# Series of unread matrix products, at many addresses, behind the last store of an encoder kernel

## The chip, the cores and the metric

The kernel runs on one core of a Trainium2 chip. The metric is the device time of one execution, in microseconds (us). TensorE (PE) multiplies; VectorE (DVE), ScalarE (ACT) and GpSimd (POOL) work on its sums and on tiles in SBUF; SyncE (SP) issues all the kernel's DMAs. PEld stands for TensorE's weight loads.

## The reference

Two layers of an encoder over 256 tokens of width 1024. Each layer adds, in turn, to the residual x: half a SwiGLU feed-forward (inner width 2816), three token mixers side by side, a cross-attention into 256 memory tokens, and half a second feed-forward; a norm ends the layer.

```python
for l in range(DEPTH):                                   # DEPTH = 2
    x = x + 0.5 * swiglu(rms_norm(x, ffn1_norm[l]), ffn1_w_in[l], ffn1_w_out[l])
    z = rms_norm(x, mix_norm[l]) @ w_mix_in[l]
    o_mla, o_swa, o_na = mla_mixer(z...), swa_mixer(z...), na_mixer(z...)
    x = x + concat(rms_norm(o_mla), rms_norm(o_swa), rms_norm(o_na)) @ w_mix_out[l]
    x = x + mem_xattn(rms_norm(x, mem_norm_x[l]), mem, ...)
    x = x + 0.5 * swiglu(rms_norm(x, ffn2_norm[l]), ffn2_w_in[l], ffn2_w_out[l])
    x = rms_norm(x, block_norm[l])
return x
```

## The kernel before

Activations lie transposed: 128 channels of a tile on the partitions, 8 such tiles (KD), and 256 tokens (T) in a row. Weights come as a stream of 332 pieces in the order of use. ScalarE rounds each piece to a four-byte type of fewer bits (float32r, "whi"), VectorE makes the rest ("wlo"). A product of high precision is then made of three rounded ones (`mm3`, lines 163 to 165), whose operands are the parts of the weights and of the activations ("...h", "...l"). Attention's scores, its transposes and its weighted values are multiplied in full precision instead; each such product is two instructions.

Sums go to eight PSUM banks of 512 columns, which `acc` hands out in turn; `slot` hands out one of ten SBUF buffers of 128x2048 four-byte numbers. The tile framework sets the semaphores: a product that begins a sum in a bank waits for whoever used the bank last, and that can be TensorE itself.

At the start, while the first data come in, four full-precision products of zeros ("idle", line 115) occupy TensorE; their sums are not read. At the end the last feed-forward's output projection ("f12o") updates x tile by tile; "end" (line 975) sums squares; GpSimd makes the factors "endr"; two transposes ("endb", line 984) spread them over the partitions; and line 987 multiplies x in five pieces, each stored to `out` by line 988. These stores are the last work of the program.

In every rounded product of this kernel both operands start 32 bytes past a multiple of 128 bytes in their partitions.

Of the kernel before, what the change touches and what calls it, by code (L numbers as in the profile page):

```python
# [10 lines left out]
F32R = mybir.dt.float32r  # L11
# [6 lines left out]
L = 2  # L18
P = 128
T = 256  # L20
# [8 lines left out]
# where in the attention's pipeline (after which head) other work is put in  # L29
# [5 lines left out]
# columns of the per-partition parameter block, per layer  # L35
G_F1, G_MIX, G_MX, G_MM, G_F2, G_BLK, G_GRP, G_CQ, G_HEAD = 0, 8, 16, 24, 32, 40, 48, 56, 59
NG = 67
# columns of the per-token (replicated) parameter block, per layer
# [4 lines left out]
def weight_plan():  # L43
    """Names and widths of the pieces of the weight stream, in the order of use."""
    plan = []
    for l in range(L):
        for name, count, width in (
            ("f1i", 2 * NJ, 1024), ("f1o", NJ, 1024), ("mc", 3, 1024), ("mb0", 4, 832), ("uq", 2, 768),
            ("mb1", 4, 1024), ("ukv", 1, 1024), ("mb2", 4, 768), ("kvk", 2, 1024), ("mo", 8, 1024),
            ("wq", 2, 1024), ("kvv", 2, 1024), ("wo", 2, 1024), ("f2i", 2 * NJ, 1024), ("f2o", NJ, 1024),  # L50
        ):
            plan += [(name, l, i, width) for i in range(count)]
    return plan


def mo_order():
    """(column tile, K tile) of the mixers' output projection: the later groups' K tiles come first."""
    o = [(i, k) for i in range(6) for k in range(4, 8)]
    o += [(i, k) for i in range(6) for k in range(4)]
    return o + [(i, k) for i in range(6, 8) for k in (4, 5, 6, 7, 0, 1, 2, 3)]  # L60
# [8 lines left out]
def encoder_kernel(ctx: ExitStack, tc: tile.TileContext, gxT, memT, wst, bparams, consts, nab, out):  # L69
    nc = tc.nc  # L70
# [39 lines left out]
    # the tensor engine's clock is gated until it has been busy for a while: busy it until the first data are there  # L110
# [43 lines left out]
    def units(kind, count):  # L154
        """Successive [128 x 128] blocks of the stream as (hi, lo)."""
        for u in range(count):
            if u % 8 == 0:
                hi, lo = piece(kind)
            o = (u % 8) * P
            yield hi[:, o : o + P], lo[:, o : o + P]  # L160
# [17 lines left out]
    class Normed:  # L178
        """hi / lo parts of (x * gain), tile by tile, and the rows' reciprocal norms.

        With pre, x stands for its own normed value with the gains pre: the rows then have two factors.
        """
# [13 lines left out]
        def _sum(self, v, keep):  # L196
            """Adds up squares, all but the last keep of them."""
            while len(v) > keep + 1:
                if len(v[0]) == 1:
                    t = tp.tile([P, T], F32, tag="sqs", bufs=3, name=self.name + "s")  # L200
                    v[0:2] = [(t, self.eng.tensor_tensor(t, v[0][0], v[1][0], ALU.add))]
                else:
                    t = v[0][0]
                    v[0:2] = [(t, self.eng.tensor_tensor(t, t, v[1][0], ALU.add))]
# [34 lines left out]
        def stats(self, r=None):  # L239
            """Means over the channels (and eps), and the factors from them: [tokens of a half, half]."""  # L240
            self.total()
            ps = acc(self.name + "ps")
            for n, v in enumerate(self.sums):
                for t in range(2):
                    s = slice(t * P, (t + 1) * P)
                    for m, q in enumerate(v):
                        nc.tensor.matmul(
                            ps[:, 2 * n + t : 2 * n + t + 1], q[0][:, s], cmean[:, 0:1],
                            start=m == 0, stop=m == len(v) - 1,
                        )  # L250
            self.m = mp.tile([P, 2], F32, tag="r", name=self.name + "m")
            nc.vector.tensor_scalar(self.m, ps[:, 0:2], EPS, None, ALU.add)
            if self.factor:
                self.r = mp.tile([P, 2], F32, tag="r", name=self.name + "r") if r is None else r
            if self.pre is None:
                if self.factor:
                    rsqrt(self.r, self.m, 2)
                return
            # both norms at once: (m2 / m + eps) ** -0.5 * m ** -0.5 = (m2 + eps * m) ** -0.5
            m2 = small(2, self.name + "m2")  # L260
            nc.vector.scalar_tensor_tensor(m2, self.m, EPS, ps[:, 2:4], ALU.mult, ALU.add)
            self.r0 = mp.tile([P, 2], F32, tag="r", name=self.name + "r0")
            rsqrt(self.r, m2, 2)
            rsqrt(self.r0, self.m, 2)

        def bcast(self):
            """The factors along the tokens, on every partition."""
            rs = [self.r] if self.pre is None else [self.r, self.r0]
            ps = acc(self.name + "pb")
            out = []  # L270
            for n, r in enumerate(rs):
                for t in range(2):
                    o = n * T + t * P
                    nc.tensor.transpose(ps[:, o : o + P], r[:, t : t + 1].to_broadcast([P, P]), ident)
                rb = tp.tile([P, T], F32, tag="rb", name=f"{self.name}rb{n}")
                nc.scalar.copy(rb, ps[:, n * T : (n + 1) * T])
                out.append(rb)
            return out
# [4 lines left out]
    def bc(ap, n):  # L283
        """[P, a, ...] -> [P, a, ..., n] by repetition."""
        return ap.unsqueeze(len(ap.shape)).to_broadcast(list(ap.shape) + [n])

# [1 line left out]
    def ffn(l, which, nx, nxt, hook=None):  # L288
# [18 lines left out]
        for j in range(NJ):  # L307
            if j == 0:
                # the tiles of x may still be in the making: two columns at once, K tile by K tile
# [49 lines left out]
    def project(nm, kind, order, nk, ah, al, nn, hooks={}, late=False):  # L359
        """x += W a in the given order of (column tile, K tile)."""  # L360
# [30 lines left out]
    class Pair:  # L391
        """Two heads whose outputs share a bank; o[:, t, cols[c], :] gets them."""
# [84 lines left out]
    def attend(heads, hooks={}, d1=AT["d1"], d2=AT["d2"]):  # L477
        """Heads in a software pipeline."""
# [16 lines left out]
    def head_factors(nm, hs, n, dim, e):  # L495
        """The heads' factors: of values that are r times what hs [P, 2, n] sums the squares of,
        r * (r ** 2 * hs / dim + eps) ** -0.5 = (hs / dim + e) ** -0.5 with e = eps / r ** 2."""
        m = small(2 * n, nm + "m")
        f = small(2 * n, nm + "f")
        t3 = lambda a: a.rearrange("p (t h) -> p t h", t=2)  # L500
        nc.vector.scalar_tensor_tensor(t3(m), t3(hs), 1.0 / dim, bc(e, n), ALU.mult, ALU.add)
        rsqrt(f, m, 2 * n)
        return t3(f)
# [8 lines left out]
    def formb(nm, kind, width, kper, xh, xl, hooks={}):  # L512
        """[tokens, width] products of the next pieces, a bank for each half of the tokens."""
# [16 lines left out]
    def head_squares(nm, ps, a, n, dim, dst):  # L530
        """Sums of squares of n heads from column a of ps into dst."""
# [12 lines left out]
    class Memory:  # L544
        """Keys and values of the memory tokens; their rows' factors serve all layers."""
# [13 lines left out]
        def steps(self, kind, n, done):  # L559
            """The next n of the 16 products (a half of the tokens, a K tile) that make keys or values."""  # L560
# [53 lines left out]
    def mixer(l, nx, mem):  # L614
        nm = f"mx{l}"
        # low-rank projections, transposed
# [17 lines left out]
        # rotary tables with the gains; the softmax scale goes on the queries' gains  # L634
# [18 lines left out]
        # rows' factors of the two latents  # L653
# [18 lines left out]
        # the rotary keys, over the factors of the latent ones  # L672
# [13 lines left out]
        # latent up-projection of the queries  # L686
# [38 lines left out]
        # heads, transposed: two to a block in the windowed and the neighbourhood group  # L725
# [19 lines left out]
        # latent up-projection of the keys and values  # L745
# [29 lines left out]
        # values of the other two groups  # L775
# [25 lines left out]
        for pr in range(2):  # L801
            # heads pr and pr + 2 lie in one block and read the two kv heads
# [80 lines left out]
    def mem_attn(l, nx, mem, nxt):  # L883
# [15 lines left out]
        # the memory tokens' values fill the time until the queries are normed  # L899
# [69 lines left out]
    # the halves of the tokens in banks of their own: only the last tile's squares are waited for  # L969
# [22 lines left out]
def _tiles(v):  # L992
    """[n] -> [128, n / 128]"""
    return v.reshape(-1, P).T


def _pack_weights(inp):
    def units_a(w, order_cols):
        """w [K, N] as [128, 128] blocks, one column tile after another, K inside."""
# [4 lines left out]
    def rows(w):  # L1004
        """w [K, N] -> [128, K / 128 * N]"""
# [5 lines left out]
    def units_in(w):  # L1011
        """Gates and values in turn; the blocks of the first four column tiles go by K tile."""
# [37 lines left out]
def _constants():  # L1050
    """Identity, rotary tables and the windowed group's biases: shapes alone decide them."""
# [17 lines left out]
def _na_bias(rel):  # L1069
    """rel [L, 4, 15, 31] gathered over (query, key); outside the window a constant."""  # L1070
# [56 lines left out]
```

## Time and profile before

| | |
|---|---|
| median of 2 runs | 1081.43 us (1080.64 and 1082.23) |
| span of the profiled execution | 1081.2 us |
| TensorE busy | 1062.2 us, 8480 products |
| VectorE, ScalarE, GpSimd busy | 718.1, 556.2, 114.3 us |
| bytes moved by DMA | 181.79 MB, 168 GB/s on average |

The span runs from the first to the last instruction of the core in one profiled execution. The page gives its shares by engine and in 40 slices of some 27 us. Products on TensorE overlap, so the pace is read from starts, or from counts in a stretch, and not from the length of one.

### The profile page before, as it was taken

The page shows a single profiled execution, that of the slowest core. Times are in us where ns is not written, and L with a number is a line of the kernel's source. Part 1 is how long each engine was busy: PE and PEld are TensorE (multiplying, and loading weights), DVE is VectorE, ACT ScalarE, POOL GpSimd, SP SyncE. Part 2 cuts the span into 40 slices and gives each one's busy share as a digit, 9 for nine tenths or more (in the row PEclk, how much of TensorE's full clock was granted, in tenths as well). Part 3 has the DMA queues.
Part 4 walks back from the last instruction along what each step waited for, and adds up shares of the span by engine and source line. Part 5 has one row for each costly group of instructions (what it writes and reads, how often), then busy time and mean ns, then how long its engine had stood idle before and what let it go on. Part 6 is the DMA issues. An engine that isn't in the chain of part 4 may idle for free.

```text
span 1081.2 us, 20915 instructions
## 1 busy us (share of the span) xinstructions
PE 1062.2 (98%) x8480; PEld 1041.3 (96%) x8480; DVE 718.1 (66%) x1249; ACT 556.2 (51%) x928; POOL 114.3 (11%) x106
## 2 busy tenths in 40 slices
PE   8999999999999999999999999999999999999996
PEld 7999999998998999999999999999889999999996
DVE  7866667678776676666658665666886776666652
ACT  5644455556563554445445444546674555444441
POOL 4000000062030400000000000001500322000000
PEclk9999999999999999999999999999999999999999
DMA  8855556555032655555555555555531526655641
GB/s 274 274 183 188 176 198 195 170 177 192 21 120 76 231 178 187 184 179 188 181 176 178 191 177 185 202 177 173 175 127 41 156 74 223 189 179 183 187 119 40
DMA packets 54529, 181.79 MB, mean 168 GB/s; under 512 B 6048, under 2 KB 8992, under 8 KB 54432
## 3 DMA queue, kind: packets, MB, share of 16 engines
q1 hardware_dynamic: 54432, 180.45, 52.3%
q8 instruction: 66, 1.08, 0.4%
q14 instruction: 31, 0.25, 0.1%
HBM read 179.38 MB, written 1.05 MB: 167 GB/s over the span
## 4 chain that ended last, share of the span: by engine, by line
PE 73%; issue 17%; DVE 4%; POOL 2%; DMA 2%; ACT 1%; SPq 0%; POOLq 0%; DVEq 0%; ACTq 0%
PE f01i L163 4%; PE f11i L163 4%; PE f01i L165 4%; PE f01i L164 4%; PE f11i L164 4%; PE f11i L165 4%; PE f02i L163 3%; PE f02i L164 3%; PE f02i L165 3%; PE f11o L165 2%; PE f11o L164 2%; PE f11o L163 2%; PE f02o L165 2%; PE f02o L164 2%; PE f02o L163 2%
## 5 line engine op out<-in xcount | busy, mean ns | idle before, releaser
L137 DVE TENSOR_TENSOR wlo<-raw,whi 128x1024 fp32r<-128x1024 f32 (+4 forms) x337 | 407.0, 1211 | 230.7 <-ACT whi L136 229.4
L136 ACT CAST whi<-raw 128x1024 fp32r<-128x1024 f32 (+4 forms) x337 | 343.5, 1022 | 384.4 <-issue 103.9
L163 PE MATMUL f11i<-n10h,whi 128*128 128x256 f32 x320 | 90.8, 284 | 0.0
L163 PE MATMUL f12i<-n21h,whi 128*128 128x256 f32 x320 | 90.7, 284 | 0.0
L163 PE MATMUL f02i<-n20h,whi 128*128 128x256 f32 x320 | 90.7, 283 | 0.0
L163 PE MATMUL f01i<-n0h,whi 128*128 128x256 f32 x320 | 90.7, 283 | 0.0
L165 PE MATMUL f01i<-n0h,wlo 128*128 128x256 f32 x320 | 90.6, 283 | 0.0
L164 PE MATMUL f02i<-n20l,whi 128*128 128x256 f32 x320 | 90.6, 283 | 0.0
L164 PE MATMUL f01i<-n0l,whi 128*128 128x256 f32 x320 | 90.5, 283 | 0.0
L164 PE MATMUL f12i<-n21l,whi 128*128 128x256 f32 x320 | 90.5, 283 | 0.0
L165 PE MATMUL f12i<-n21h,wlo 128*128 128x256 f32 x320 | 90.5, 283 | 0.0
L165 PE MATMUL f02i<-n20h,wlo 128*128 128x256 f32 x320 | 90.5, 283 | 0.0
L164 PE MATMUL f11i<-n10l,whi 128*128 128x256 f32 x320 | 90.5, 283 | 0.0
L165 PE MATMUL f11i<-n10h,wlo 128*128 128x256 f32 x320 | 90.5, 283 | 0.0
L164 PEld LDWEIGHTS f12i<-n21l,whi 128*128 128x128 f32 x320 | 61.4, 192 | 0.0
L164 PEld LDWEIGHTS f02i<-n20l,whi 128*128 128x128 f32 x320 | 61.4, 192 | 0.0
L164 PEld LDWEIGHTS f01i<-n0l,whi 128*128 128x128 f32 x320 | 61.4, 192 | 0.0
L165 PEld LDWEIGHTS f02i<-n20h,wlo 128*128 128x128 f32 x320 | 61.4, 192 | 0.0
L163 PEld LDWEIGHTS f02i<-n20h,whi 128*128 128x128 f32 x320 | 61.4, 192 | 0.0
L164 PEld LDWEIGHTS f11i<-n10l,whi 128*128 128x128 f32 x320 | 61.4, 192 | 0.0
L165 PEld LDWEIGHTS f01i<-n0h,wlo 128*128 128x128 f32 x320 | 61.4, 192 | 0.0
L163 PEld LDWEIGHTS f12i<-n21h,whi 128*128 128x128 f32 x320 | 61.4, 192 | 0.0
(1025 smaller groups left out, 2977.0 us busy)
## 6 DMA issues: line engine op xcount, KB each, us to landing
raw<-in_w SPq DMA_DIRECT2D x311, 512.0 KB, 4.3
raw<-in_w SPq DMA_DIRECT2D x12, 384.0 KB, 3.5
raw<-in_w SPq DMA_DIRECT2D x8, 416.0 KB, 3.2
kv0mt<-in_mem SPq DMA_DIRECT2D x8, 128.0 KB, 4.2
kv1mt<-in_mem SPq DMA_DIRECT2D x8, 128.0 KB, 3.3
gx<-in_gx SPq DMA_DIRECT2D x3, 256.0 KB, 7.2
out<-gx SPq DMA_DIRECT2D x3, 256.0 KB, 2.8
gx<-in_gx SPq DMA_DIRECT2D x1, 323.0 KB, 3.0
```

The lines of the kernel that those rows point to most:

```text
L136: ins = nc.scalar.copy(hi[:, a:b], r[:, a:b])
L137: nc.vector.tensor_tensor(lo[:, a:b], r[:, a:b], hi[:, a:b].bitcast(F32), ALU.subtract)
L163: nc.tensor.matmul(ps, ah, bh, start=first, stop=False)
L164: nc.tensor.matmul(ps, ah, bl, start=False, stop=False)
L165: return nc.tensor.matmul(ps, al, bh, start=False, stop=last)
```

## The change

Behind the loop of the last stores, two more buffers of 128x2048 are taken, sr and mr, and VectorE casts x into both. TensorE then multiplies parts of sr (as weights) with parts of mr (as streamed data). "heat" is one sum of 24 products with 512 columns. After it come 110 sums, the series. Their names carry a shift in bytes of the weights (w) and of the streamed data (m): 70 series of 7 products with 256 columns (za: w of 0, 32, 64, 96, m from 0 to 480 in steps of 32, and at w = 0 six more m that are multiples of 8), 32 of 5 with 512 (zb: the same w, m in steps of 64) and 8 of 5 with 384 (zc: w = 0). Within a series the weights move on by 128 columns from product to product. No sum is read. All other hunks of the diff take comments and docstrings away.

```diff
@@ -988,28 +988,55 @@
         nc.sync.dma_start(out[:, a:b, :], v)
 
 
-# ---- host layout ----
+    sr = slot([P, 8, T], F32R, "sr")
+    mr = slot([P, 8, T], F32R, "mr")
+    for d_ in (sr, mr):
+        nc.vector.tensor_copy(d_, x)
+    st, mv = sr.rearrange("p k t -> p (k t)"), mr.rearrange("p k t -> p (k t)")
+
+    def series(name, w, m, n, reps):
+        ps = acc(name)
+        for i in range(reps):
+            o = w // 4 + (i * 128) % 1024
+            nc.tensor.matmul(
+                ps[:, 0:n], st[:, o : o + 128], mv[:, m // 4 : m // 4 + n], start=i == 0, stop=i == reps - 1
+            )
+
+    series("heat", 0, 0, 512, 24)
+    for w in (0, 32, 64, 96):
+        for m in range(0, 512, 32):
+            series(f"zaw{w}m{m}n", w, m, 256, 7)
+    for m in (8, 16, 24, 40, 48, 56):
+        series(f"zaw0m{m}n", 0, m, 256, 7)
+    for w in (0, 32, 64, 96):
+        for m in range(0, 512, 64):
+            series(f"zbw{w}m{m}n", w, m, 512, 5)
+    for m in range(0, 512, 64):
+        series(f"zcw0m{m}n", 0, m, 384, 5)
```

On VectorE, at the end of the program, the order of the instructions (gx holds x, endb the factors):

```order
 L987 TENSOR_TENSOR gx<-gx,endb 128x256 x2
 L987 TENSOR_TENSOR gx<-gx,endb 128x512 x3
-L1122 UNCONDITIONAL_BRANCH
+L994 CAST sr<-gx 128x2048
+L994 CAST mr<-gx 128x2048
+L1149 UNCONDITIONAL_BRANCH
```

The two casts stand behind the last multiplication of x; nothing ahead of them moved.

On TensorE, at the end of the program, with what each waits for (DVE_49 and PE_49 are the semaphores that VectorE and TensorE raise; the 102 series behind these eight go on like the last of them):

```order
+L1001 MATMUL heat<-mr,sr 128x512 [waits DVE_49]
+L1001 MATMUL heat<-mr,sr 128x512 x23
+L1001 MATMUL zaw0m0n<-mr,sr 128x256 x7
+L1001 MATMUL zaw0m32n<-mr,sr 128x256 x7
+L1001 MATMUL zaw0m64n<-mr,sr 128x256 x7
+L1001 MATMUL zaw0m96n<-mr,sr 128x256 x7
+L1001 MATMUL zaw0m128n<-mr,sr 128x256 x7
+L1001 MATMUL zaw0m160n<-mr,sr 128x256 x7
+L1001 MATMUL zaw0m192n<-mr,sr 128x256 [waits PE_49]
+L1001 MATMUL zaw0m192n<-mr,sr 128x256 x6
+L1001 MATMUL zaw0m224n<-mr,sr 128x256 [waits PE_49]
+L1001 MATMUL zaw0m224n<-mr,sr 128x256 x6
```

Before, TensorE's program ends with the transposes of line 984; now the products of line 1001 follow them, the first behind the casts. The orders on ScalarE, GpSimd and SyncE are as before.

## Rows read from the trace of the kernel before

**Rows 1.** The page: engines' busy time with share and instructions, and TensorE's clock by slices.
```profile
PE 1062.2 (98%) x8480; PEld 1041.3 (96%) x8480; DVE 718.1 (66%) x1249; ACT 556.2 (51%) x928; POOL 114.3 (11%) x106
...
PEclk9999999999999999999999999999999999999999
```
**Rows 2.** Windows, last feed-forward: stretch; length, TensorE busy (products), clock; DMA share, GB/s.
```profile
1000.00:1060.00 60.00, 60.00 (x503) 1.00 0.47 138
```
**Rows 3.** Timeline of the program's end: start, length, engine, instruction; idle before.
```profile
1073.03 0.69 POOL L169 TENSOR_TENSOR endr<-endm,nhalf 128x2 f32<-128x2 f32 x1 [174.12 <-DVE endm L980]
1073.77 0.19 PEld L984 LDWEIGHTS endb<-ident,endr 128*128 128x128 f32 x2 [1.11 <-POOL endr L169]
1074.25 2.55 DVE L987 TENSOR_TENSOR gx<-gx,endb 128x256 f32<-128x256 f32 x5 [1.30 <-PE endb L984]
1074.70 2.46 SPq L988 DMA_DIRECT2D out<-gx  x5
```
**Rows 4.** Windows: from 1075 us to the end, columns as in rows 2.
```profile
1075.00:1081.20 6.20, 0.00 (x0) 0.57 0.52 170
```
**Rows 5.** VectorE's groups by form: busy us, mean ns of one, idle before.
```profile
L848 DVE TENSOR_SCALAR mx0o<-mx0o,mx0or 128x256 f32<-128x256 f32 x4 | 1.2, 349 | 0.4 <-POOL mx0or L169 0.3
L848 DVE TENSOR_SCALAR mx0o<-mx0o,mx0or 128x512 f32<-128x512 f32 x2 | 0.9, 483 | 0.8 <-POOL mx0or L169 0.8
L210 DVE TENSOR_SCALAR n21h<-gx 128x256 fp32r<-128x256 f32 x4 | 1.4, 344 | 0.0
L137 DVE TENSOR_TENSOR wlo<-raw,whi 128x1024 fp32r<-128x1024 f32 x308 | 380.6, 1239 | 219.3 <-ACT whi L136 218.0
```
**Rows 6.** Timeline of TensorE at the program's start.
```profile
1.26 3.78 PE L115 MATMUL idle<-idle 128*128 128x256 f32 x8 [1.26 <-DVE idle L112]
...
6.26 1.06 PE L318 MATMUL f01s<-n0l,whi 128*128 128x256 f32 x4
7.11 0.79 PE L318 MATMUL f01s<-n0h,wlo 128*128 128x256 f32 x4
7.80 0.74 PE L318 MATMUL f01s<-n0h,whi 128*128 128x256 f32 x4
8.37 0.64 PE L318 MATMUL f01s<-n0l,whi 128*128 128x256 f32 x4
8.85 0.40 PE L318 MATMUL f01s<-n0h,wlo 128*128 128x256 f32 x2
```
**Rows 7.** Windows: the first mixer's products of 512 columns, columns as in rows 2.
```profile
224.22:234.68 10.46, 10.46 (x47) 1.00 0.59 197
```
**Rows 8.** Timeline of TensorE: products of 384 columns, first and fourth of four.
```profile
239.37 0.33 PE L524 MATMUL mx0mb<-whi,nx0h 128*128 128x384 f32 x1
...
239.89 0.33 PE L524 MATMUL mx0mb<-whi,nx0h 128*128 128x384 f32 x1
```
**Rows 9.** Timeline of TensorE: the mixers' output, into the third column tile.
```profile
297.65 0.28 PE L165 MATMUL mx0mo<-mx0oh,wlo 128*128 128x256 f32 x1
297.77 0.28 PE L163 MATMUL mx0mo<-mx0oh,whi 128*128 128x256 f32 x1
```
**Rows 10.** Timeline of TensorE: one head's scores in full precision.
```profile
270.77 1.03 PE L434 MATMUL mx0ml01sc<-mx0kT,mx0qT 96*128 96x256 f32 x4
271.64 0.60 PE L461 MATMUL mx0na10pt<-ident,mx0na10p 128*128 128x128 f32 x4
```
**Rows 11.** Timeline of TensorE: products of 416 columns, four of seven.
```profile
211.95 0.36 PE L526 MATMUL mx0mb<-whi,nx0l 128*128 128x416 f32 x1
212.15 0.35 PE L524 MATMUL mx0mb<-whi,nx0h 128*128 128x416 f32 x1
...
212.91 0.35 PE L525 MATMUL mx0mb<-wlo,nx0h 128*128 128x416 f32 x1
213.09 0.35 PE L526 MATMUL mx0mb<-whi,nx0l 128*128 128x416 f32 x1
```
**Rows 12.** DMA issues of the page: KB each, median us from issue to landing.
```profile
out<-gx SPq DMA_DIRECT2D x3, 256.0 KB, 2.8
```

## The prediction, made before the result

> **What bounds the kernel now.** I read the page's engine shares first, then TensorE's pace in a stage where it is never idle, then the end of the timeline, and last the rows nearest to what is added. TensorE is busy for 1062.2 of 1081.2 us with its clock near full speed in every slice, and no other engine comes near [rows 1]. In the feed-forward stages the pace is even: 60 us hold 503 products, some three of which only reach in over the edges, so 0.120 us each [rows 2]. The end is another picture. TensorE's last work, two transposes, starts at 1073.77 with their weight load; VectorE then multiplies and SyncE stores behind it, until 1076.80 and 1077.16, and the span closes at 1081.2 [rows 3]. So TensorE stands idle through the last 7 us, and from 1075.0 to the end its mean granted clock is 0.57: it falls from 1.0 to the half level about 0.9 us into that stretch [rows 4].
>
> The reader should see that nothing in this program runs behind the added work. Whatever TensorE is given there can hide only under the store's landing and the closing checks, from some 1077 to 1081 us. All else comes on top.
>
> **The change part by part.** The removed comments and docstrings produce no instruction. VectorE gets two casts of 128x2048 behind its last multiplication; TensorE gets 714 products behind its last transpose: 24 of 512 columns ("heat"), 70 series of 7 with 256 columns, 32 series of 5 with 512, 8 series of 5 with 384. All have weights of 128 columns, of the same rounded four-byte type as the feed-forward's. No engine's earlier order moves, and SyncE's queue is unchanged, so the part before 1076.8 us costs nothing more.
>
> *Casts.* The trace has no cast of this size on VectorE. The nearest rows are the one-input TENSOR_SCALARs from and to SBUF: 349 ns for 256 columns and 483 for 512, so 133 ns for 256 more, also where the output is the rounded type (344) [rows 5]. For 2048 that is 483 + 6 x 133 = 1281 ns, 2.56 us for both. The other end is the two-input subtraction, 1239 ns for 1024 [rows 5]: twice that twice is 4.96 us. I take the first, whose operands are of the casts' kind: 1076.80 + 2.56 + 0.05 from a release to the weight load (endr ends at 1073.72, the load begins at 1073.77 [rows 3]) lets the first product start at **1079.4**; the other end gives 1081.8.
>
> *Heat.* By then the clock has been down for over 3 us [rows 4], so heat begins cold. What cold costs is seen at the start of the program: four f01s products of 256 columns need 0.2125 us each (6.26 to 7.11), where four a little later need 0.12 (8.37 to 8.85) [rows 6]. 256 array steps at 1.2 GHz are 0.2133 us, so it is the half clock; 512 are 0.427, and that is what a cold product of 512 columns takes, against 0.2275 warm (10.46 us for 47, one reaching over the edge [rows 7]). The pace changes between the group at 7.11 us and the one at 7.80, some 6.2 us after the first product at 1.26. With the same 6.2 us, 14.5 of the 24 are cold and 9.5 warm: 6.2 + 2.2 = **8.4 us**. Bounds: 5.5 us if all are warm, 10.3 if all are cold.
>
> *Series.* At the pace of before: 490 x 0.120 = 58.8 [rows 2]; 160 x 0.2275 = 36.4 [rows 7]; 40 x 0.174 = 7.0, from three steps between 239.37 and 239.89 [rows 8]. Together **102.2 us**. Each new series needs a bank, and from the eighth on waits on TensorE's own semaphore for the series eight places back; that one is over some 5 to 9 us earlier. Mixers' output column tiles already wait so, one with its first product at 297.77, 0.12 us behind the last of the sum before, as within a sum [rows 9]. I cost these waits at nothing; their cover is the eight banks. Nobody reads the sums, so no evacuation holds a bank.
>
> What is open is the address. Every rounded product of before has weights and stream starting 32 bytes past a multiple of 128 bytes; the tiles sr and mr start there too, but the series shift the weights by 0 to 96 bytes and the stream by 0 to 480. Paces of before contain a surcharge: 256 columns at 2.4 GHz are 106.7 ns, and 120 were taken; 512 are 213.3, and 227 were taken. So 13.3 ns whatever the width. Four-byte products in full precision need two steps a column, and show hardly any: four of mx0ml01sc with 512 steps each stand from 270.77 to 271.64, 0.2175 each against 213.3 ns [rows 10]. Nor has f01s it at the half clock: 0.2125 against 213.3 ns for 256 columns at 1.2 GHz [rows 6]. So the surcharge looks like one of reading the stream at full rate, which an address could change. That it can is hinted at by 416 columns: from one product to the next it is 0.18 to 0.20 us, though nothing but the addresses differs [rows 11]. I therefore bound the address's part from both sides by the same 13.3 ns: a third of the 690 products losing about 10.8 of it gives -2.5 us, a quarter paying it twice +2.3. I take zero, since widths in whole multiples of 128 show one pace at all addresses that occur.
>
> The Trainium skill's page "TensorE: Matmul & The Clock Gate", section "Back-to-back issue gap", gives N/2.4 + 2.5 ns for a warm product. As an estimate by that page the series would take 490 x 109 + 160 x 216 + 40 x 162.5 ns = 94.5 us. The trace agrees for full-precision products (0.217) and disagrees for rounded ones (0.120, not 0.109).
>
> *Closing.* The last product lasts some 0.16 us past its pace (0.33 against 0.174 [rows 8]). Then come the closing checks: before, the last of the five stores is issued in the last fifth of 1074.70 to 1077.16 and lands 2.8 us after that begins [rows 3, 12], at 1079.5, and 1081.2 is 1.7 us later. The stores' checks will be over, so I take 1.0, between 0.5 and 1.7.
>
> *Sum.* 1079.4 + 8.4 + 102.2 + 0.2 + 1.0 = 1191.2 us of span, against 1081.2 of the profiled execution. The median shown, 1081.43, is 0.2 above that span: **1191.4 us**, 10.2% more.
>
> **The rivals.** (a) *The surcharge belongs to the old addresses.* If a start 32 bytes past a 128-byte multiple causes it, and most other starts don't, the pace falls to that of the full-precision products, width/2.4 + 2.5: 7.7 us less, 1183.7. For it: the reading explanation above. Against: a quarter of the 256-wide streams at most would start on a multiple of 128, none of the wider ones, and then only 112 x 10.8 ns = 1.2 us go, which lies inside my range. It needs a finer rule on addresses to reach 1183.7.
>
> (b) *Weights and stream collide.* At some differences of address a load of weights and the running stream could want the same part of the memory, and three quarters of the 690 could pay a second 13.3 ns: +6.9 us, 1198.3; all of them paying two more, 1209.8. For it: 416 columns are uneven [rows 11]. Against: the mean there, 0.188 over the five steps from 212.15 to 213.09, is within 2 ns of width/2.4 + 13.3. The Trainium skill's page "SBUF — State Buffer", section "Who interferes with whom", says that TensorE reads streams and weights through two independent ports, which would rule this rival out; no run here shows ports.
>
> (c) *The clock stays down.* With half the clock through all series: 10.3 + 490 x 0.213 + 160 x 0.427 + 40 x 0.32 = 196 us, 1277. It decides if the stream of products is too thin to be granted the full clock; but the same products keep it at 1.0 over the whole kernel [rows 1, 2].
>
> (d) *Nothing is added.* The sums are unread; if a compiler behind the built program drops products that nobody reads, TensorE ends as before and only the casts remain, under the store: 1081 to 1082, not slower. For it: nothing in the profile; against: the four idle products at the start are unread too, and they are in the trace, eight instructions strong [rows 6]. It would decide only if the drop took whole series.
>
> **How the numbers follow.** The forecast has 0.72, (a) 0.08, (b) 0.14, (c) 0.04, (d) 0.02. The range takes the forecast's bounds: down 2.9 (heat warm at once) and 2.7 (addresses, closing) to 1185.8, up 1.9 (heat cold), 2.4 (casts) and 2.3 (addresses) to 1198.0; that takes in part of (b). About 2% is what a measurement of this kernel tells from no change, 21.6 us; all cases but (d) are far beyond it: slower 0.98, same 0.02, faster 0.
>
> **What would show it.** Two casts of 1.28 us each from 1076.8; a first heat product at about 1079.4 with a half clock, and a pace that turns from 0.427 to 0.2275 after some 6 us; series of 256 at 0.120, of 512 at 0.2275, of 384 at 0.174, without a gap between them; under 1.3 us from the last product to the end. Wrong in (a) or (b) would show as series whose paces differ with the numbers in their names, wrong in (c) as a clock row near 0.5 in the added stretch. What would mislead me most is a dependence on addresses of more than one surcharge, since the trace holds a single class of them.

## The result, and the profile after

The changed kernel takes 1192.63 us, the median of two runs (1191.15 and 1194.11), against 1081.43 before: a ratio of 1.1032 with a 95% interval of 1.1011 to 1.1053. The forecast was 1191.4 with a range of 1185.8 to 1198.0.

The page of the kernel after, with the engines' busy time, the line that answers to [rows 1]:

```profile
PE 1171.9 (99%) x9194; PEld 1141.9 (96%) x9194; DVE 721.2 (61%) x1251; ACT 555.7 (47%) x928; POOL 113.2 (10%) x106
```

TensorE has 714 more products and 109.7 us more busy time; VectorE has two more instructions and 3.1 us. All added products ran.

The timeline of the same kernel's end (start, length, engine, instruction, count; in brackets the idle time before and what ended it), which answers to [rows 3]:

```profile
1071.58 0.70 POOL L169 TENSOR_TENSOR endr<-endm,nhalf 128x2 f32<-128x2 f32 x1 [172.98 <-DVE endm L980]
...
1072.80 2.54 DVE L987 TENSOR_TENSOR gx<-gx,endb 128x256 f32<-128x256 f32 x5 [1.30 <-PE endb L984]
1075.38 1.23 DVE L994 CAST sr<-gx 128x2048 fp32r<-128x2048 f32 x1
1076.52 1.22 DVE L994 CAST mr<-gx 128x2048 fp32r<-128x2048 f32 x1
1077.80 8.62 PE L1001 MATMUL heat<-mr,sr 128*128 128x512 f32 x24 [5.03 <-DVE mr L994]
```

Everything up to the factors "endr" ended 1.45 us earlier in this execution than in the profiled one of before (1071.58 against 1073.03). The casts take 1.23 and 1.22 us and start 1.14 apart, so the second begins while the first is still shown as running. TensorE waits 5.03 us for them, and then nothing holds it up.

Windows of the same kernel, one for each kind of series (stretch; length, TensorE busy with its products, granted clock; DMA share, GB/s):

```profile
1077.80:1084.00 6.20, 6.20 (x15) 0.50 0.02 4
1084.00:1086.25 2.25, 2.25 (x11) 1.00 0.00 0
1086.25:1144.15 57.90, 57.90 (x491) 1.00 0.00 1
1144.15:1181.30 37.15, 37.15 (x163) 1.00 0.00 1
1181.30:1188.20 6.90, 6.90 (x41) 1.00 0.00 0
```

And the timeline's last row, the last of eight series of 384 columns:

```profile
1187.41 1.04 PE L1001 MATMUL zcw0m448n<-mr,sr 128*128 128x384 f32 x5
```

The counts hold a product or two that reach in over an edge. Heat is cold at first and takes 8.45 us in all. The 490 products of 256 columns follow in 57.90 us, 118.2 ns each; the 160 of 512 in 37.15, 232.2 each; the 35 of 384 columns from 1181.30 to 1187.41 need 174.6 ns each, which makes 6.98 us for all 40 and puts their end, by pace, at 1188.28. TensorE is busy in the whole of every window: no series begins with a wait. To the end of the span at 1189.4 it is 1.1 us more: the last product shows as running until 1188.45, and 0.95 us follow.

The total is as forecast, but two of its paces are not those of before: 118.2 against 120 ns [rows 2], and 232.2 against 227.5 [rows 7]. Inside the series single products go from 113 to 125 ns and from 225 to 240, and the pattern repeats with the difference of the two start addresses, m - w. Timeline of the same kernel, pairs of neighbouring series:

```profile
1091.23 0.97 PE L1001 MATMUL zaw0m192n<-mr,sr 128*128 128x256 f32 x7
1092.04 0.98 PE L1001 MATMUL zaw0m224n<-mr,sr 128*128 128x256 f32 x7
...
1117.66 1.00 PE L1001 MATMUL zaw64m192n<-mr,sr 128*128 128x256 f32 x7
1118.49 0.98 PE L1001 MATMUL zaw64m224n<-mr,sr 128*128 128x256 f32 x7
1119.32 0.97 PE L1001 MATMUL zaw64m256n<-mr,sr 128*128 128x256 f32 x7
1120.13 0.98 PE L1001 MATMUL zaw64m288n<-mr,sr 128*128 128x256 f32 x7
```

From one start to the next, the stream at m = 192 takes 0.81 us for seven products with the weights at 0, and 0.83 with the weights at 64. With the weights at 64 it is m = 256, again 192 further on, that takes 0.81. The experiments are mostly about the two small errors, which the sum hides.

### The profile page after: what moved, and what is told of

The parts are those of the page before. It is cut to its first block, busy times and chain, and to the rows that moved or that the text cites. A ratio compares the mean times of both kernels' runs of the same rounds, so it can differ in the third digit from the quotient of the medians.

```text
span 1189.4 us, 22346 instructions
## 1 busy us (share of the span) xinstructions
PE 1171.9 (99%) x9194; PEld 1141.9 (96%) x9194; DVE 721.2 (61%) x1251; ACT 555.7 (47%) x928; POOL 113.2 (10%) x106
## 4 chain that ended last, share of the span: by engine, by line
PE 76%; issue 16%; DVE 4%; POOL 2%; DMA 1%; ACT 1%; SPq 0%; DVEq 0%; POOLq 0%; ACTq 0%
PE f01i L163 3%; PE f11i L163 3%; PE f01i L165 3%; PE f01i L164 3%; PE f11i L164 3%; PE f11i L165 3%; PE f02i L163 3%; PE f02i L164 3%; PE f02i L165 3%; PE f11o L165 2%; PE f11o L164 2%; PE f11o L163 2%; PE f02o L165 2%; PE f02o L164 2%; PE f02o L163 2%
## 5 line engine op out<-in xcount | busy, mean ns | idle before, releaser
L163 PEld LDWEIGHTS f01i<-n0h,whi 128*128 128x128 f32 x320 | 61.4, 192 | 0.0
```

Source lines behind the costliest of these rows:

```text
L163: nc.tensor.matmul(ps, ah, bh, start=first, stop=False)
```

## The experiments

*Settling* holds that a change of width or of address upsets a steady pace, which comes back after some products whatever the addresses are. *Distance* holds that the pace depends on how far in bytes the stream starts behind the weights, taken modulo 256. *Boundary* holds that the start of a sum in another bank costs something. *Load* says of the 13.3 ns which a product takes above width/2.4 that it comes from the weight load beside it, and not from the stream alone. Where no ratio stands beside a time, it is that of a single execution.

**All series at one address.** In each call the two shifts become zero:

```diff
-            series(f"zaw{w}m{m}n", w, m, 256, 7)
+            series(f"zaw{w}m{m}n", 0, 0, 256, 7)
```

> All 110 series read weights and stream at the first address; counts, widths, banks and waits stay. Settling theory (a change of width or of the distance between the two addresses upsets the pace, which then settles within some ten products on a multiple of 13.3 ns): series of 256 at 120 ns (58.8 us for all, where the change took 57.9), of 512 at 227 after the first ten (36.4 us, where it took 37.1), of 384 at 173.5. Distance theory (each distance has a pace of its own, whatever came before): 256 at 119.0, 512 at 230.5, 384 at 175.4, the means of the change's products at distance zero. Boundary theory (each new series costs, by its wait or its bank): 118, 232 and 175 as in the change. All three: 1191 to 1194 us, the same time as the change within 0.1%.

Measured: 1191.73 us, ratio to before 1.1018 (1.1000 to 1.1036). Windows of this kernel, series of 256 and of 512 columns, and then the timeline of its first series of 512:

```profile
1087.17:1145.96 58.79, 58.79 (x492) 1.00 0.00 1
1145.96:1182.25 36.29, 36.29 (x162) 1.00 0.00 1
```

```profile
1145.96 1.32 PE L1001 MATMUL zbw0m0n<-mr,sr 128*128 128x512 f32 x5
1147.12 1.30 PE L1001 MATMUL zbw0m64n<-mr,sr 128*128 128x512 f32 x5
1148.25 1.29 PE L1001 MATMUL zbw0m128n<-mr,sr 128*128 128x512 f32 x5
```

58.79/490 is 120.0 ns and 36.29/160 is 226.8: the pace of before at 256 columns, and within 0.7 ns of it at 512. These are settling's numbers; the 119.0 and 230.5 that distance had taken from the short series did not come. The first series of 512 takes 1.16 us from start to start and the next one 1.13: five unsteady products behind the change of width, then none, although each series begins another bank. Boundary falls. Both paces move together with the addresses, by +0.9 and -0.9 us, so the two errors of the forecast belong to the addresses.

**Long series.** Each address is held for 61, 20 or 10 products:

```diff
-    for w in (0, 32, 64, 96):
-        for m in range(0, 512, 32):
-            series(f"zaw{w}m{m}n", w, m, 256, 7)
...
+    for m in range(0, 256, 32):
+        series(f"zaw0m{m}n", 0, m, 256, 61)
+    for m in range(0, 256, 32):
+        series(f"zbw0m{m}n", 0, m, 512, 20)
+    for m in range(0, 256, 64):
+        series(f"zcw0m{m}n", 0, m, 384, 10)
```

> Nearly the same number of products, in 20 long series: 8 of 61 with 256 columns, 8 of 20 with 512, 4 of 10 with 384, each at one distance of the addresses (0 to 224 bytes). Settling theory: after some ten products every series stands at 120, 226.7 or 173.3 ns, whatever its distance; 512 columns in all 36.6 to 36.9 us for 160, 256 columns 58.5 for 488. Distance theory: the paces stay apart to the end of a series, 256 between 116.2 (192 bytes) and 119.2, 512 between 230.5 and 233.4. Boundary theory: 227 for 512 at all distances from the second product on.

Measured: 1190.81 us. Timeline of TensorE, the last two series of 256 columns and the first three of 512:

```profile
1129.67 7.08 PE L1001 MATMUL zaw0m192n<-mr,sr 128*128 128x256 f32 x61
1136.58 7.38 PE L1001 MATMUL zaw0m224n<-mr,sr 128*128 128x256 f32 x61
1143.80 4.70 PE L1001 MATMUL zbw0m0n<-mr,sr 128*128 128x512 f32 x20
1148.34 4.83 PE L1001 MATMUL zbw0m32n<-mr,sr 128*128 128x512 f32 x20
1153.01 4.75 PE L1001 MATMUL zbw0m64n<-mr,sr 128*128 128x512 f32 x20
```

From start to start, 61 products at distance 192 take 6.91 us, 113.3 ns each, and at 224 7.22 us, 118.4. Twenty of 512 take 4.54 us at distance 0 and 4.67 at 32, 227.0 and 233.5 each. Within some ten products each series falls into a pattern that repeats, as settling says; but the mean of the pattern differs with the distance, as the other theory says. Each was half right.

**Weights of 64 columns.** Half the columns are loaded; the products of the series are half as tall:

```diff
-    def series(name, w, m, n, reps):
+    def series(name, w, m, n, reps, c=64):
...
-                ps[:, 0:n], st[:, o : o + 128], mv[:, m // 4 : m // 4 + n], start=i == 0, stop=i == reps - 1
+                ps[0:c, 0:n], st[:, o : o + c], mv[:, m // 4 : m // 4 + n], start=i == 0, stop=i == reps - 1
```

> In all series but heat, products load 64 columns of weights in place of 128 (and fill 64 partitions of the sums); streams, counts and addresses stay. If the 13.3 ns above width/2.4 come from the weight load that runs beside the stream, half a load takes about half of them off: 112 to 113 ns for 256 columns, 220 for 512, 55 us and 35 us, the whole 3 to 5 us shorter. If they belong to the stream alone: 118, 232 and 175 as in the change, and the same time.

Measured: 1191.48 us. The means are 117.5, 230.6 and 173.5 ns, where the changed kernel has 118.2, 232.2 and 174.6. Taken over all addresses the load's size is worth under 0.7 us; at distance 0 with 256 columns the products settled at about 113.3 ns, half of the surcharge less. With only seven products at each address that is not enough; the run on the size of the load, below, has more.

**The casts alone.** No added product runs:

```diff
-    series("heat", 0, 0, 512, 24)
-    for w in (0, 32, 64, 96):
...
```

> The two casts are kept, all 714 products are left out. By the prediction's account the casts end about 1.0 us after the last store is issued and before it lands, so they are hidden: 1081 to 1082 us, ratio 1.000 within 0.002. If they delay the closing (their rival: VectorE's end is late), up to 2.5 us more, 1084.

Measured: 1081.7 us, ratio 1.0002 (0.9992 to 1.0011). Timeline of this kernel's end:

```profile
1076.79 1.22 DVE L994 CAST mr<-gx 128x2048 fp32r<-128x2048 f32 x1
```

Its span closes at 1080.1, 2.1 us behind the second cast, so the casts cost nothing without products behind them. Like the changed kernel it had "endr" early, at 1071.60.

**A scan of distances.** 38 series of 32 products with 256 columns, by steps of 8 bytes:

```diff
+    for m in range(0, 272, 8):
+        series2(f"zam{m}n", 0, m, 256, 32)
+    for m in (180, 188, 196, 204):
+        series2(f"zam{m}n", 0, m, 256, 32)
```

(`series2` is `series` with the number of weight columns as one more argument; it stands for the old series in this and two later kernels.)

> The tail holds 38 series of 32 products with 256 columns; weights stay at the first address, the stream is shifted by 0 to 264 bytes in steps of 8, and by 180, 188, 196 and 204. If the settled pace is a function of the distance between stream and weights alone, with a period of 256 bytes: 0 and 256 settle on 120, 8 and 264 on the same as each other, 192 on 113.3, 32 to 160 and 224 repeat the means of the long series before (117.6 to 120.4); between 160 and 224 the pace falls towards 192 and none lies below 109 (256 columns at 2.4 GHz and the 2.5 ns of the full-precision products). If what was seen at 192 came from the order of the series, it does not come back: 117 to 119 there.

Measured: 1233.1 us with its 1216 products. Timeline of TensorE, four of the series in a row:

```profile
1176.86 3.81 PE L1009 MATMUL zam192n<-mr,sr 128*128 128x256 f32 x32
1180.51 4.00 PE L1009 MATMUL zam200n<-mr,sr 128*128 128x256 f32 x32
1184.35 3.97 PE L1009 MATMUL zam208n<-mr,sr 128*128 128x256 f32 x32
1188.16 4.05 PE L1009 MATMUL zam216n<-mr,sr 128*128 128x256 f32 x32
```

Over 32 products, settling included, 192 has 114.1 ns, 200 has 120.0, 208 119.1 and 216 121.6. Once settled, 0, 8, 40, 104, 188, 256 and 264 all have 120.0, 160 has 117.3, 112 and 192 have 113.3, and none is below that. 256 is like 0 and 264 like 8, so the period is 256 bytes as far as tried. Two things came otherwise than expected: the dip at 192 is narrow (188 and 196 have 120) and no slope, and there is a second one at 112. Distance 32 came out at 116.7 ns here and at 117.8 among the long series, so one distance can have more than one pattern.

**The size of the load.** Series of 24, with four sizes of weights, two distances, four widths:

```diff
+    for c in (128, 96, 64, 32):
+        for m in (0, 192):
+            for n in (256, 240, 224, 512):
+                series2(f"zac{c}m{m}n{n}n", 0, m, n, 24, c)
```

> 32 series of 24 products: weights of 128, 96, 64 and 32 columns, distance 0 or 192 bytes, streams of 256, 240, 224 and 512 columns. If the surcharge comes from the weight load that runs beside the stream, at distance 0 and 256 columns it goes down with the load: 120, 116 to 117, 113, 110. If it comes from the stream alone: 120 at every load. Streams of 240 columns: an added 13.3 ns gives 113.3; a pace locked to multiples of 13.3 ns gives 120 or 106.7.

Measured: 1196.98 us. Timeline of TensorE (128*64 is 64 columns of weights):

```profile
1086.07 3.04 PE L1009 MATMUL zac128m0n256n<-mr,sr 128*128 128x256 f32 x24
1088.94 2.85 PE L1009 MATMUL zac128m0n240n<-mr,sr 128*128 128x240 f32 x24
1091.63 2.83 PE L1009 MATMUL zac128m0n224n<-mr,sr 128*128 128x224 f32 x24
1094.30 5.66 PE L1009 MATMUL zac128m0n512n<-mr,sr 128*128 128x512 f32 x24
1099.80 2.99 PE L1009 MATMUL zac128m192n256n<-mr,sr 128*128 128x256 f32 x24
...
1140.46 2.89 PE L1009 MATMUL zac64m0n256n<-mr,sr 128*64 128x256 f32 x24
1143.19 2.72 PE L1009 MATMUL zac64m0n240n<-mr,sr 128*64 128x240 f32 x24
```

At distance 0 a product of 256 columns takes 2.87/24 = 119.6 ns with 128 columns of weights and 2.73/24 = 113.8 with 64; with 96 it is 116.2. So far it goes down with the load, as expected. But with 32 columns it settles at 117.8 and not at 110, and with 512 streamed columns at distance 0 every smaller load is slower than the full one (230 to 232 ns settled against 226.7); at distance 192, where the full one has 233.3, the smaller ones have 228 to 233. A load that simply takes its share of time away would do neither. A smaller load also fills fewer partitions of the sum, and this run does not separate the two. At distance 192 with full weights the settled pace at 256 columns was now 117.8, not 113.3 as in the scan.

The narrower streams say more about the load. With full weights at distance 0, 240 columns take 2.69/24 = 112 ns and 224 take 2.67/24 = 111, although width/2.4 is 6.7 ns less for the second; with 96 columns of weights 224 take 104. So with a full load the pace stops following the width near 111 ns, not far under the 113.3 that is the lowest for 256 columns. The load seems to set a floor there; no run tried it at narrower streams.

**A fill before heat.** Twelve unread full-precision products stand on TensorE behind the two transposes, to keep it busy while VectorE casts:

```diff
+    fill = acc("fill")
+    for i in range(12):
+        nc.tensor.matmul(fill[:, 0:T], ident, rope.rearrange("p a b -> p (a b)").unsqueeze(1).to_broadcast([P, 2, P]), start=True, stop=True)
```

> Twelve unread full-precision products (24 instructions of 0.216 us) stand between the last transposes and the added series, so that TensorE is not idle while the casts run; the rest is the change. If heat's first part is slow because the clock fell in that gap: the clock stays at 1.0 from the encoder into the series, all 24 heat products take 227 ns, 5.5 us in place of 8.46, and the time falls by 2.5 to 3.0 us, to 1188.5 to 1190. If a stream is slow at its begin for another reason: again about 8.4 us and 1192.

Measured: 1192.33 us. Timeline of TensorE, and then windows of the same kernel:

```profile
1073.98 8.12 PE L995 MATMUL fill<-rope,ident 128*128 128x256 f32 x24
1081.75 5.82 PE L1004 MATMUL heat<-mr,sr 128*128 128x512 f32 x24
```

```profile
1073.00:1079.50 6.50, 6.00 (x15) 0.50 0.47 161
1079.60:1087.40 7.80, 7.80 (x36) 1.00 0.01 3
```

The clock was already at its half level when the fill began, and the fill itself ran the cold part. Heat behind it has a clock of 1.00 and takes 5.66 us from its start to the first series at 1087.41, where 24 x 0.2275 is 5.5. So all but some 0.2 us of heat's excess is the clock. The saving that was expected did not come: the fill held heat back from 1079.2, where the second cast ends, to 1081.75. In this execution the clock fell at about 1072.8, ahead of the last transposes at 1073.50 (its mean is 1.00 from 1071 to 1072 us and 0.88 in the next one); in the profiled one of before it fell only at 1075.9, behind them [rows 4]. What a fill at this place can save may thus change from one execution to the next, and this is a single one.

**Upsets.** Eight times at each of four distances: first a series of one to three wider products as an upset, then 36 products:

```diff
+    for d in (0, 192, 112, 160):
+        for p in range(8):
+            series(f"zkd{d}p{p}n", 0, 32 * p, (384, 512)[p % 2], 1 + p % 3)
+            series2(f"zad{d}p{p}n", 0, d, 256, 36)
```

> The tail holds 32 series of 36 products with 256 columns: eight each at the distances 0, 192, 112 and 160. Ahead of each stand 1 to 3 products of 384 or 512 columns at changing distances, which upset the pace in different ways. If the pace has several settled patterns at one distance and the upset picks one: at 192 some series settle on 113.3 and some on 117.7, each to its end; at 0 all on 120. If the settled pace follows from the distance alone: all eight at 192 on 113.3, all at 112 on 113.3, all at 160 alike.

Measured: 1237.07 us. Timeline of TensorE, two of the eight series at distance 192 and one at 112:

```profile
1129.48 4.40 PE L1009 MATMUL zad192p1n<-mr,sr 128*128 128x256 f32 x36
1134.24 4.25 PE L1009 MATMUL zad192p2n<-mr,sr 128*128 128x256 f32 x36
...
1161.15 4.24 PE L1009 MATMUL zad112p0n<-mr,sr 128*128 128x256 f32 x36
```

Less the last product's own 0.28 us, 4.25 is 35 steps of 113.4 ns and 4.40 is 117.7. At 192 four series settled on the one and four on the other; at 112 all eight end on 113.3; at 0 all eight have 120.0; at 160 two settled on 117.3 and six on 118.7. So a distance allows one or several steady patterns, and what went before chooses.

**The kernel before, with its activations at other distances.** In the kernel before, weights and streams of the feed-forward lie at distance 0. Moving one pool ahead of the activations' buffers makes it 160, and 32 bytes of padding more make it 192; nothing is added behind the last store (the lines on `gap` and `shift` are those for 192):

```diff
     wp = ctx.enter_context(tc.tile_pool(name="wp", bufs=7))
+    mp = ctx.enter_context(tc.tile_pool(name="mp", bufs=9))
+    gap = ctx.enter_context(tc.tile_pool(name="gap", bufs=1))
     sp = ctx.enter_context(tc.tile_pool(name="sp", bufs=10))
     tp = ctx.enter_context(tc.tile_pool(name="tp", bufs=2))
-    mp = ctx.enter_context(tc.tile_pool(name="mp", bufs=9))
...
+    shift = gap.tile([P, 8], F32, name="shift")
+    nc.gpsimd.memset(shift, 0.0)
```

> The kernel before, without any added product. Only the order of the SBUF pools differs, with a pad of 32 bytes: the activation tiles now start 192 bytes (modulo 256) past the weight tiles. 6937 rounded products of 256 columns then run beside weight loads at distance 192, 266 at 64, those of 384 and 512 columns at 64. Distance theory: 6937 x 6.7 ns = 46 us less, minus 0.3 for the 512 wide, as far as TensorE is the bound: 1035 to 1042 us, ratio 0.957 to 0.964. Rival: the chain that splits the weights (2.26 us of ScalarE and VectorE for each piece, which TensorE would use up in 2.72 us in place of 2.88) or the weights' DMA falls behind: half of it, 1058. Rival: the effect belongs to the tail's two tiles alone: 1081.

> The version with its activation tiles 192 bytes past the weight tiles, less the pad of 32 bytes: the same order of pools, distance 160. If the distance of the addresses sets the gain: the long series at 160 settled on 117.1 to 118.7 ns, so 6937 products gain 1.3 to 2.9 ns each, 9 to 20 us, and those of 512 columns (now at 96) lose up to 0.9: 1062 to 1073 us, ratio 0.981 to 0.992. If the order of the pools did it: 1048 as at 192.

Distance 112 cannot be had by order alone: the buffers were made 256 bytes longer and used from 16 bytes on, the pool of constants was moved behind the weights' with 64 bytes of padding, and to make room two kinds of temporary tiles got one buffer fewer:

```diff
     def slot(shape, dt, name):
-        return sp.tile(shape, dt, tag="S", name=name)
+        t = sp.tile([P, 2112], dt, tag="S", name=name)
+        n = int(np.prod(shape[1:]))
+        v = t[:, 4 : 4 + n]
...
-        return tp.tile([P, T], F32, tag="b1", bufs=9, name=name)
+        return tp.tile([P, T], F32, tag="b1", bufs=8, name=name)
```

> The kernel before with the activation buffers 256 bytes longer and used from 16 bytes on, the pool order changed and a pad of 64 bytes, so that the activations stand 112 bytes (modulo 256) past the weights; one buffer less of each of two temporary kinds makes room. 6843 rounded products of 256 columns run at distance 112, 266 at 144, 260 of 384 and 512 columns at 144. If 112 has a single settled pattern of 113.3 ns, as all eight of its series had, the whole gain of 6843 x 6.7 = 46 us comes, less the same waits as at 192: 1034 to 1042 us, and no feed-forward stage stands at 117.7. If the two patterns of 192 belong to the kernel's waits rather than to the distance, some stages stand on another pace again: about 1048. If the smaller number of buffers delays the feed-forward's ends: above 1048.

A control has the same longer buffers, used from their first byte on, and the same smaller counts, with all pools in their old places and so at distance 0:

```diff
-        v = t[:, 4 : 4 + n]
+        v = t[:, 0:n]
```

> The same longer buffers and the same smaller number of temporaries, with the old pool order and no offset: distance 0 for all products of 256 columns. The buffers' cost by itself: the time of before within 0.3% (1079 to 1085 us), 120 ns in all feed-forward stages. If the longer buffers, and not the distance, bring the gain of the version at 112: 1040.

| distance | time, us | ratio to before (95%) |
|---|---|---|
| 160 | 1070.17 | 0.9895 (0.9878 to 0.9911) |
| 192 | 1048.62 | 0.9689 (0.9673 to 0.9705) |
| 112, fewer buffers | 1045.03 | 0.9651 (0.9634 to 0.9668) |
| 0, fewer buffers | 1085.11 | 1.0025 (1.0014 to 1.0036) |

The groups of one tile in TensorE's instructions: count, shortest/median/longest in ns, first and last start. The last feed-forward's output projection, the third of its products that multiplies "f12ah" by "whi", stands in this order: before, distance 160, 192, 112, the control. At 160 and 192 the row for "f11o" stands ahead of it, since it has another pace.

```profile
L163 PE MATMUL f12o<-f12ah,whi x176: 283/283/283, 1007.2 to 1070.2; 128*128 128x256 f32 x176
```

```profile
L163 PE MATMUL f11o<-f11ah,whi x176: 277/280/282, 659.3 to 720.9; 128*128 128x256 f32 x176
L163 PE MATMUL f12o<-f12ah,whi x176: 277/281/283, 994.7 to 1057.0; 128*128 128x256 f32 x176
```

```profile
L167 PE MATMUL f11o<-f11ah,whi x176: 281/281/282, 647.1 to 708.9; 128*128 128x256 f32 x176
L167 PE MATMUL f12o<-f12ah,whi x176: 276/276/277, 976.9 to 1036.4; 128*128 128x256 f32 x176
```

```profile
L172 PE MATMUL f12o<-f12ah,whi x176: 275/275/275, 973.7 to 1033.2; 128*128 128x256 f32 x176
```

```profile
L168 PE MATMUL f12o<-f12ah,whi x176: 283/283/283, 1010.1 to 1073.1; 128*128 128x256 f32 x176
```

From the first start to the last are 525 products: 63.0 us before and in the control (120.0 ns), 62.3 at 160 (118.7), 59.5 at 192 and at 112 (113.3). At 192 "f11o" took 61.8 (117.7), the second of the two patterns of the upsets, and the input projection "f11i" ahead of it was on that one too. The two lost some 6.3 us by it, which is the main reason why 192 gained 33 us and not the 39 to 46 expected. The kernel at 160 came out as expected, and its stages too stand on the two paces that its series had: "f11o" takes 61.6 us (117.3 ns), "f12o" 118.7. At 112 all four output stages have 113.3. That kernel missed its expectation by some 3 us. Its control shows one reason: longer slots and fewer buffers cost 2.5 us by themselves. The timeline and a window of the kernel at 112 show the other, at the head of "f02i":

```profile
356.24 1.01 PE L256 MATMUL n20ps<-cmean,n20s 128*128 128x1 f32 x4 [2.04 <-POOL n20s L213]
```

```profile
356.20:363.00 6.80, 6.76 (x31) 0.50 0.81 286
```

TensorE had waited 2.04 us there for GpSimd's part of a norm. Behind the norm's four narrow products, 27 of "f02i" then ran at half the clock: 5.9 us, where at 113.3 ns they would take 3.1. Before, that wait is 1.10 us and the clock is 1.00 all through the stage; at 160 it is 1.51, and at 192 1.99, where 15 products behind it ran at the half clock. The faster TensorE is, the longer it waits there. Against its own control, distance 112 is worth 40 us.

## Why the prediction held, point by point

**What bounds the kernel, and what is added on top: right.** No engine's earlier work changed, TensorE's queue ran through without a gap, and the added time came on top of the old end. Rival (d) is out by the count of products, rival (c) by the clock of 1.00 from 1084.00 on.

**Casts: right, by the lower bound's rows.** 1.281 us each were forecast from one-input operations [rows 5], 1.23 and 1.22 came, and they overlap by 0.09. With the factors "endr" 1.45 us earlier in this execution, heat began at 1077.80 instead of 1079.4. That they hide under the store when nothing follows is shown by the kernel with the casts alone.

**Heat: right, and closer than could be known.** 8.45 us against 8.4. The cold products cost 0.427 us, and the pace turned after some 6.2 us, as at the program's start [rows 6]; the kernel with a fill shows that a granted clock of 1.00 takes the excess away. But in six other executions without a fill heat took from 7.18 to 8.10 us, with 8 to 12 cold products where this one had 14. So the 6.2 us are not a constant, and the agreement to 0.05 us is luck.

**Series: the sum is right, its terms are not.** 102.2 us were forecast, 102.0 measured: za is 0.9 too high (118.2 ns instead of 120), zb 0.75 too low (232.2 instead of 227.5), zc right. At one address the series of 256 and 512 columns take 58.79 and 36.29 us and show the paces of before, so the step that failed is *the address at zero*: the address counts, with opposite signs at the two widths, and the signs happened to cancel. The reason given for zero, one pace at all addresses that occur, could not bear it: in the feed-forward of before all products lie at distance 0. The bounds of -2.5 and +2.3 held either part.

**Its reason was wrong.** I took the 13.3 ns for a surcharge of reading the stream at full rate. The size of the weight load changes it (119.6 to 113.8 ns at distance 0), and so does the distance between the two; the stream alone can't explain either. Rival (b), a meeting of load and stream, was right in that the two affect each other, and wrong as a price: the differences found go from -6.7 to +1.3 ns at 256 columns and from 0 to about +7.5 at 512, not a second surcharge upward. That they want the same part of the memory, as it supposed, is not shown. The Trainium skill's page "SBUF — State Buffer", section "Who interferes with whom", lets TensorE read streams and weights through two independent ports. No run here shows ports, but the prediction was wrong to let this speak against the rival: the paces depend on both addresses together, and the measurement decides. Rival (a) fails: no distance reached width/2.4 + 2.5 ns, which for 256 columns is 109.2; the lowest settled pace is 113.3. That figure is from the section "Back-to-back issue gap" of the Trainium skill's page "TensorE: Matmul & The Clock Gate", which gives it for an isolated product, and no rounded product here came down to it.

**Banks: right.** At one address there is no cost at the start of a sum, with 110 sums in eight banks.

**Closing and what lies around the span.** 1.1 us from the last product's pace to the end, against 0.2 and 1.0. The profiled execution took 1191.15 us for a span of 1189.4, 1.75 more; I had taken 0.2, by setting the median of before against the span of its profiled execution. The kernel with the casts alone also has 1.76 (1081.86 for a span of 1080.1), so by these the profiled execution of before stood at some 1083 us, over its median. It was a late one inside, too: over the ten profiled executions in which nothing ahead of "endr" was changed, "endr" starts between 1071.13 and 1073.05 us, and at 1073.03 in that of before. The 1.55 us too little around the span and the 1.45 too much inside it nearly cancel, since the profiled execution after happened to be an early one; that is luck.

**What stays open.** Why the load and the stream disturb each other is not shown: no run has a record of ports or of memory banks. So is why one distance has one steady pattern (112) and others two (160, 192), and why smaller loads are slower at 512 columns and distance 0. Distance 112 without the cost in buffers was not tried, nor a fill issued ahead of the transposes.

## What to carry to other kernels

A product of few columns with a new weight load each time has a pace that belongs to the addresses, not only to its width: where such products bound a kernel, look at the starts of weights and streams modulo 256 bytes, try a few distances, and read the settled pace from a stage of hundreds of products. Here that placement took 1082 us to 1049 by the order of the pools and 32 bytes. And work that is appended behind a kernel's end begins on an engine that has gone cold: cost its first microseconds at the half clock, from rows at that clock.

## What was not expected of the hardware

- Rounded four-byte products of 256 columns have settled paces from 113.3 ns (distances 112 and 192) to 121.3 (216), with 120.0 at 0; products of 512 have their best, 226.7, at 0 and up to 234 elsewhere. Distance 192, the best for 256 columns together with 112, is a poor one for 512 (233).
- At distance 192 two steady paces exist, 113.3 and 117.7 ns, and a stage of 528 products stays on the one that it fell into ("f12o" on the first, "f11o" on the second). Distance 160 has two as well, 117.3 and 118.7, in the series and in the kernel.
- Halving the weight columns took 120 to 113.3 ns at distance 0 and 256 columns, and a quarter of them gave 117.8. With full weights 240 and 224 columns both take 111 to 112.
- The granted clock falls at different points of the same work: 2.1 us behind the start of the last transposes in one execution, ahead of them in another.
- A cast of 2048 columns from four-byte to rounded four-byte numbers takes VectorE 1.22 us, 0.6 ns a column.
